# Layer B: emptying the key and query accumulators behind the next product's first two splits, and a second place for the LayerNorm rows

## The chip, the cores and the metric

The kernel runs on one core of one Trainium2 chip. A core has engines that work side by side, each through its own list of instructions in order: TensorE (PE, matrix products; PEld is its loading of weights), VectorE (DVE), ScalarE (ACT), GpSimd (POOL, all but unused here) and SyncE (SP, which issues the transfers from memory). They wait for one another through semaphores. The metric is the device time of one execution in microseconds (us), lower is better.

## The reference

A decoder trunk with two layers, 256 tokens and width 2048, all in 32-bit floats. Layer A is a state-space mixer. After it one set of keys and values is made from its output x; layer B is an attention with three head groups g, each with its own window and dilation, eight heads of 128 in each.

```python
k, v   = split(x @ kv_w)                  # 2048 -> 3072 keys, 3072 values
shift, scale, gate = split(silu(c) @ ada_w[1] + ada_b[1])   # 2048 -> 3 x 2048
h      = x * (1 + scale) + shift
q, z   = split(h @ b_in_w)                # 2048 -> 3072 queries, 1024 gate
o      = merge over g of softmax(q_g k_g' / sqrt(128) + alibi) v_g
out    = layer_norm(2**0.5 * x + (1 + gate) * ((o * silu(z)) @ b_out_w), ln_g, ln_b)
```

## The kernel before

**Products in split precision.** Every large product is computed as three: a weight piece `raw` (128 x 1024, 512 KB) is loaded, ACT copies it to a rounded high part `whi` (line 99), DVE subtracts to get the low part `wlo` (line 101), and PE multiplies high by high, high by low and low by high. There are six buffers for `raw`, four for `whi` and four for `wlo`.

**The stretch that the change touches** is the second half of the program.

- First come the values of the first half of the heads (`wv`, chunks of eight pieces by `tm_chunk`; evicted by `evict_v`, two ACT copies of 128 x 512, line 856).
- Then twelve key products (`wk`), each one call of `cm_wide`. It takes four pieces q = 0..3, called p0 to p3 below. A piece gives 16 matmuls: for each of four slices of the contraction two of 128 x 512 with the high part (line 173), then two of 128 x 256 with the low part (line 176). The results stand in a pair of PSUM accumulators `acc`; four accumulators exist, so one product fills a pair while the other pair is emptied. Emptying one takes an ACT copy (line 181) and a DVE addition (line 182), 128 x 256, and this twice per product.
- Then three more chunks of `wv`. Meanwhile the input of layer B, h, is made in place of x, tile by tile for 16 tiles (`htmp`: ACT line 923, DVE line 924; then the split into `actT`: ACT line 225, DVE line 226). A tile of x may only be overwritten when PE has read it for the last time, in the last `wv` chunk.
- Then six query products (`wbin`, `cm_wide` again), an attention over four heads, six more query products, the second attention, and the end.

**Background work.** `jobs` is a list from which `background` takes a job after a piece (`rate`). During keys and values every second piece takes one column of the adaLN matrix: a 1 MB load `araw` and a DVE dot product (line 279, two buffers). During the first queries each piece takes one step of `weigh` (line 943): the residual u is multiplied with the LayerNorm weight and then increased by the LayerNorm bias, for four column blocks n and two token blocks b. The rows of weight and bias for one n stand in one tile `pT` (128 x 1024), broadcast from memory by two transfers of 256 KB; the tile has one place, so the rows of n + 1 are loaded when n is done.

**What sets the order.** The functions write the instructions down; a scheduler then lays them out, engine by engine, by its own estimate of when each could start, so an instruction may come ahead of others that the code writes first. `tc.issue_after(x)` binds it: what is inside stands behind x. `upcoming`, `begin_next`, `first_or` and `behind_next` start the next product early: if `upcoming` holds its source, its p0 is loaded and split before the last piece of the running product, and the emptying stands behind that split. In layer A `upcoming` is filled; in layer B it is empty in this kernel, so `begin_next` does nothing there and `behind_next` binds nothing.

Of the kernel before, what the change touches and what calls it, by code (L numbers as in the profile page):

```python
# [9 lines left out]
F32 = mybir.dt.float32  # L10
F32R = mybir.dt.float32r
I32 = mybir.dt.int32
AF = mybir.ActivationFunctionType
# [5 lines left out]
P = 128  # L19
L = 256  # L20
D = 2048
# [6 lines left out]
NG = 3  # L28
# [21 lines left out]
def trunk(ctx, tc, xT, x, c, par, cst, bias, lnrow, ada, wdt, win, wxs, wout, wk, wv, wbin, wbout, out):  # L50
    nc = tc.nc
    V, S, T, PO = nc.vector, nc.scalar, nc.tensor, nc.gpsimd
# [9 lines left out]
    def bcast(dst, src, off=0):  # L62
        nc.sync.dma_start(dst, bass.AP(tensor=src.tensor, offset=src.offset + off,
                                       ap=[[0, P], [1, dst.shape[-1]]]))
# [37 lines left out]
        return hi.rearrange("p (k n) -> p k n", k=2), lo.rearrange("p (k n) -> p k n", k=2)  # L102

    jobs, latest, copied, pin = [], [], [], [None]
    upcoming, ready = [], []

    def first_or(src, q):

        return ready.pop() if ready else split(load_piece(src[q]))
# [7 lines left out]
    def behind_next():  # L117

        stack = ExitStack()
        if ready:  # L120
            stack.enter_context(tc.issue_after(copied[-1].ins))
            stack.enter_context(tc.issue_after(latest[-1].ins))
        return stack
# [34 lines left out]
            background(*rate)  # L158
        return ps

    def cm_wide(src, dst, rate=(0, 1), moving=None):

        both, high = moving or (lambda kt: xp[:, kt], lambda kt: xhi[:, kt, :])
        ps = acc_pair()
        for q in range(KT // 4):
            w = first_or(src, q)
            if q == KT // 4 - 1:
                begin_next()
            hi, lo = (t.rearrange("p k n -> p (k n)").rearrange("p (k n) -> p k n", k=4) for t in w)
            for k in range(4):  # L170
                kt = 4 * q + k
                for n in range(2):
                    T.matmul(ps[n], hi[:, k, n * P:n * P + P], both(kt), start=kt == 0, stop=False,  # L173
                             skip_group_check=True)
                for n in range(2):
                    T.matmul(ps[n][:, 0, :], lo[:, k, n * P:n * P + P], high(kt), start=False, stop=kt == KT - 1,  # L176
                             skip_group_check=True)
            background(*rate)
        with behind_next():
            for n in range(2):  # L180
                S.activation(dst[:, n, :], ps[n][:, 1, :], AF.Copy)
                V.tensor_tensor(dst[:, n, :], ps[n][:, 0, :], dst[:, n, :], op=ALU.add)

    def tiles(ps):
        return [ps[n // 2][:, n % 2, :] for n in range(4)]
# [20 lines left out]
    def tm_chunk(src, ahi, alo, nk=KT, rate=(0, 1), k0=0, pre=None, split_end=0):  # L206

        ps = tm_pair()
        n = nk // 2 - split_end
        for q in range(k0 // 2, n):  # L210
            if pre:
                pre(q)
            w = first_or(src, q)
            if q == nk // 2 - 1:
                begin_next()
            tm_piece(src, q, ps, ahi, alo, k0, nk, w=w)
            background(*rate)
        held = [(q, split(load_piece(src[q]))) for q in range(n, nk // 2)]
        for b in range(2):
            for q, w in held:  # L220
                tm_mults(q, w, ps, ahi, alo, k0, nk, (b,))
        return ps
# [63 lines left out]
    def gate_out(layer):  # L286

        ada_bias(layer, slice(0, KT), slice(2, 3))
        pt = aux.tile([P, 512], F32, name="aux")[:KT, :P]
        T.transpose(pt, mod[layer][:, :, 2], ident)  # L290
        row = sm.tile([KT, P], F32, name="row", bufs=1)
        V.tensor_copy(row, pt)
        nc.sync.dma_start(gated[layer].rearrange("(k p) -> k p", p=P), row)
# [24 lines left out]
    with ExitStack() as cA:  # L318
# [15 lines left out]
        with ExitStack() as cS:  # L334
# [78 lines left out]
            with ExitStack() as c0:  # L413
# [42 lines left out]
                for row in ("b4:0. b6:0. h z2:0. b2:0 x1:0 h", "b2:1. x1:1. z1:0 z1:1. z4:0 h h",  # L456
# [3 lines left out]
                    for w in row.split():  # L460
                        if w == two:
                            n = -2 if sum(o[0] == -2 for o in order) == sum(o[0] == -1 for o in order) else -1
# [99 lines left out]
            R = (1, 10)  # L562
# [284 lines left out]
    kv, vt = {}, {}  # L847
# [4 lines left out]

    def evict_v(hq, g, ps):
        vt[hq, g] = place(3 * hq + g if hq == 0 else 9 + g, [P, 2, 512])
        for b in range(2):
            S.activation(vt[hq, g][:, b, :], ps[b], AF.Copy)

    with ExitStack() as cL:
        pl = cL.enter_context(tc.tile_pool(name="pl", bufs=3))

        vps = [tm_pair(), tm_pair()]
        def high(i, b):
            for k in range(2):
                kt = 2 * (i // 2) + k
                for w in first_v[i]:
                    T.matmul(vps[i % 2][b], hx(kt)[:, b * P:b * P + P], w[:, k, :], start=kt == 0 and w is first_v[i][0],  # L866
                             stop=False)

        def low(i, b):
            for k in range(2):  # L870
                T.matmul(vps[i % 2][b], lx(2 * (i // 2) + k)[:, b * P:b * P + P], first_v[i][0][:, k, :], start=False,
                         stop=False)

        end, _ = x_quad(0)
        with tc.issue_after(end.ins):
            for n in range(1, 4):
                normalise(0, 512 * n, 512 * n + 512)
        for i in range(4):
            high(i, 0)
        for i in range(4):  # L880
            if i == 2:
                _, tile4 = x_quad(1)
                for n in range(1, 4):
                    normalise(1, 512 * n, 512 * n + 512)
            low(i, 0)
        for i in range(4):
            high(i, 1)
            if i == 2:
                x_tile(4)
                x_tile(5)  # L890
        for i in range(4):
            low(i, 1)
        for q in range(2, KT // 2):
            if q < KT // 2 - 1:
                x_tile(2 * q + 2)
                x_tile(2 * q + 3)
            for j in range(2):
                w = split(load_piece(wv[2 * j][q]), after=tile4.ins if q == 2 else None)
                tm_mults(q, w, vps[j], hx, lx, 0, KT, range(2))
        for g in range(2):  # L900
            evict_v(0, g, vps[g])

        R = (1, 2)
        pin[0] = latest[-1].ins
        with tc.issue_after(tile4.ins):
            state[0] = 0
            queue(pl, cols1[11:])
            jobs.append(lambda: gate_out(1))
            evict_v(0, 2, tm_chunk(wv[4], hx, lx, rate=R))
            for hq in range(2):  # L910
                for g in range(NG):
                    kv[hq, g] = place(3 + 3 * hq + g, [P, 4, L])
                    for w in range(2):
                        cm_wide(wk[2 * (2 * g + hq) + w], kv[hq, g][:, 2 * w:2 * w + 2, :], rate=R)
            for g in range(NG):
                evict_v(1, g, tm_chunk(wv[1 + 2 * g], hx, lx, rate=R))
            drain()
            late = latest[-1].ins

        ada_bias(1, slice(0, KT), slice(0, 2))  # L920
        for kt in range(KT):
            t = pl.tile([P, L], F32, name="htmp")
            S.activation(t, xhi[:, kt, :].bitcast(F32), AF.Identity, bias=shift(1, kt), scale=scale(1, kt))
            V.scalar_tensor_tensor(t, xlo[:, kt, :].bitcast(F32), scale(1, kt), t, op0=ALU.mult, op1=ALU.add)
            split_act(xhi[:, kt, :], xlo[:, kt, :], t)
    cQ = ctx.enter_context(ExitStack())
    pc2 = cQ.enter_context(tc.tile_pool(name="pc2", bufs=2))
# [4 lines left out]
    gmask = bs[:, CG:CG + 640]  # L932
    R = (0, 1)

    def weigh(n, b, i):
        if b == 0 and i == 0:
            t = pc2.tile([P, 1024], F32, name="pT", bufs=1)
            lnr[n] = [t[:, 512 * j:512 * j + 512] for j in range(2)]
            for j in range(2):
                bcast(lnr[n][j], lnrow, j * D + 512 * n)  # L940
        cs_ = slice(512 * n, 512 * n + 512)
        with tc.issue_after(late):
            V.tensor_tensor(u[b][:, cs_], u[b][:, cs_], lnr[n][i], op=(ALU.mult, ALU.add)[i])

    lnr = {}
    state[0] = 0
    jobs.extend(lambda n=n, b=b, i=i: weigh(n, b, i) for n in range(4) for i in range(2) for b in range(2))

    def queries(hq):
        qq = [pc2.tile([P, 4, L], F32, name=f"q{g}") for g in range(NG)]  # L950
        for g in range(NG):
            for w in range(2):
                cm_wide(wbin[2 * (2 * g + hq) + w], qq[g][:, 2 * w:2 * w + 2, :], rate=(1, 1))
        return qq

    def attend(hq, qq):
# [91 lines left out]
    for n in range(2):  # L1048
        ps = tm_chunk(wbout[n], *og, nk=H)
# [12 lines left out]
    ps = [tm_pair() for _ in range(2)]  # L1062
# [140 lines left out]
```

## Time and profile before

| | us |
|---|---|
| three runs, median (lowest to highest) | 1247.58 (1247.24 to 1248.12) |
| the profiled execution, its own time | 1247.47 |
| its span, first to last instruction | 1245.7 |
| PE busy | 1216.8 (98%) |
| PE weight loads busy | 1043.1 (84%) |
| DVE busy | 1029.4 (83%) |
| ACT busy | 702.5 (56%) |

The profiled execution is 0.11 us from the median, so numbers of its trace can be set against either. Times in the trace count from the start of the span. The stretch in question lies between 771 and 1041 us: keys to about 907, values to 974, first queries to 1041. A table by windows gives busy time of each engine in a stretch and the number of its instructions in brackets; an engine's timeline gives start, duration, line, operands and, in square brackets, the idle time just before and what ended it. In a timeline several equal instructions in a row are drawn together (x2), with one duration from the first start to the last end; consecutive matmuls overlap.

### The profile page before, as it was taken

Reading aid. Unit: us, or ns where it says so; the run is one execution under the profiler, and the core shown is the slowest. Engines: PE = TensorE matmul, PEld = TensorE weight load, DVE = VectorE, ACT = ScalarE, POOL = GpSimd, SP = SyncE. Lnnn points to the kernel's source line nnn. Section 1 sums busy time; section 2 is a strip of 40 time slices with the busy share of each in tenths; the row PEclk is TensorE's granted clock in tenths of the full one; section 3 lists DMA queues with packets and bytes.
Section 4 is the critical chain, followed back from the end, with each engine's and each line's share of the span. In section 5 each row is a group of like instructions: output and inputs, shape, how many; then the busy total and the mean of one; then the engine's idle time right before and its main releaser. Section 6 shows DMA issues by size and latency. Waiting matters only on the chain.

```text
span 1245.7 us, 18736 instructions
## 1 busy us (share of the span) xinstructions
PE 1216.8 (98%) x7086; PEld 1043.1 (84%) x7086; DVE 1029.4 (83%) x1454; ACT 702.5 (56%) x1045; POOL 0.2 (0%) x4
## 2 busy tenths in 40 slices
PE   4999999999999999999999999999999999999997
PEld 4989998898888888888888788888888888888886
DVE  6999986999987989899768678879888867658777
ACT  3645477868597789654335554443445644445631
POOL 0000000000000000000000000000000000000000
PEclk9999999999999999999999999999999999999999
DMA  9999977687556456699998569988998774463751
GB/s 381 422 421 422 421 266 252 223 287 263 211 186 220 155 183 194 227 334 351 337 333 288 187 213 375 363 329 344 354 382 314 238 242 135 136 204 117 232 175 67
DMA packets 80586, 335.88 MB, mean 270 GB/s; under 512 B 9104, under 2 KB 9328, under 8 KB 67696
## 3 DMA queue, kind: packets, MB, share of 16 engines
q1 hardware_dynamic: 80496, 334.69, 74.6%
q8 instruction: 55, 0.90, 0.3%
q14 instruction: 35, 0.29, 0.1%
HBM read 332.47 MB, written 2.18 MB: 269 GB/s over the span
## 4 chain that ended last, share of the span: by engine, by line
PE 86%; DVE 6%; DMA 4%; ACT 2%; issue 2%; SPq 0%; DVEq 0%; ACTq 0%
PE acc L173 21%; PE acc L199 12%; PE acc L200 12%; PE acc L198 12%; PE acc L176 11%; PE acc L144 3%; PE acc L146 3%; PE acc L145 3%; DMA araw<-in_ada 2%; DVE araw L279 2%; DVE wlo L101 2%; PE py L657 1%; ACT whi L99 1%; PE acc L866 1%; PE aux L969 1%
## 5 line engine op out<-in xcount | busy, mean ns | idle before, releaser
L99 ACT ACTIVATE whi<-raw 128x1024 fp32r<-128x1024 f32 x392 | 411.2, 1058 | 369.9 <-PE acc L200 135.9
L101 DVE TENSOR_TENSOR wlo<-raw,whi 128x1024 fp32r<-128x1024 f32 x392 | 472.7, 1220 | 135.9 <-ACT whi L99 128.5
L173 PE MATMUL acc<-actT,whi 128*128 128x512 f32 x1280 | 405.3, 397 | 0.0
L176 PEld LDWEIGHTS acc<-actT,wlo 128*128 128x128 f32 x1280 | 239.1, 188 | 59.1 <-DVE wlo L101 4.3
L199 PE MATMUL acc<-wlo,actT 128*128 128x512 f32 x656 | 257.5, 393 | 0.6 <-DVE wlo L101 0.5
L176 PE MATMUL acc<-actT,wlo 128*128 128x256 f32 x1280 | 253.4, 279 | 1.7 <-DVE wlo L101 1.2
L198 PE MATMUL acc<-whi,actT 128*128 128x512 f32 x656 | 253.1, 394 | 0.0
L279 DVE SCALAR_TENSOR_TENSOR araw<-araw,cb__72 128x2048 f32<-128x2048 f32 x96 | 219.3, 2285 | 12.1 <-DMA araw<-in_ada 11.8
L173 PEld LDWEIGHTS acc<-actT,whi 128*128 128x128 f32 x1280 | 195.9, 189 | 0.4
L200 PE MATMUL acc<-whi,actT 128*128 128x512 f32 x432 | 168.9, 391 | 0.0
L199 PEld LDWEIGHTS acc<-wlo,actT 128*128 128x128 f32 x656 | 123.2, 188 | 28.0 <-DVE wlo L101 3.1
L198 PEld LDWEIGHTS acc<-whi,actT 128*128 128x128 f32 x656 | 122.5, 188 | 24.2
L144 PE MATMUL acc<-actT,whi 128*128 128x256 f32 x384 | 109.1, 288 | 17.6 <-ACT actT L446 17.4
L145 PE MATMUL acc<-actT,whi 128*128 128x256 f32 x384 | 109.4, 287 | 0.0
L146 PE MATMUL acc<-actT,wlo 128*128 128x256 f32 x384 | 107.5, 287 | 0.9 <-DVE wlo L101 0.9
L200 PEld LDWEIGHTS acc<-whi,actT 128*128 128x128 f32 x432 | 81.1, 188 | 16.6
L144 PEld LDWEIGHTS acc<-actT,whi 128*128 128x128 f32 x384 | 74.5, 195 | 18.6 <-ACT actT L446 17.6
L200 PE MATMUL acc<-whi,ylo 128*128 128x512 f32 x224 | 87.6, 391 | 0.0
L145 PEld LDWEIGHTS acc<-actT,whi 128*128 128x128 f32 x384 | 75.1, 196 | 0.3
L146 PEld LDWEIGHTS acc<-actT,wlo 128*128 128x128 f32 x384 | 73.9, 196 | 1.3 <-DVE wlo L101 1.3
L200 PEld LDWEIGHTS acc<-whi,ylo 128*128 128x128 f32 x224 | 42.1, 188 | 8.5
L615 ACT ACTIVATE seg<-cbc,cumT 128x128 f32<-128x128 f32 x128 | 41.0, 389 | 4.9 <-DVE wlo L101 2.3
(273 smaller groups left out, 1108.8 us busy)
## 6 DMA issues: line engine op xcount, KB each, us to landing
araw<-in_ada SPq DMA_DIRECT2D x96, 1024.0 KB, 7.5
raw<-in_win SPq DMA_DIRECT2D x112, 512.0 KB, 6.8
raw<-in_wout SPq DMA_DIRECT2D x64, 512.0 KB, 5.8
raw<-in_wbin SPq DMA_DIRECT2D x64, 512.0 KB, 3.7
raw<-in_wxs SPq DMA_DIRECT2D x48, 512.0 KB, 4.6
raw<-in_wv SPq DMA_DIRECT2D x48, 512.0 KB, 6.7
raw<-in_wk SPq DMA_DIRECT2D x48, 512.0 KB, 7.1
cbc<-cumd SPq DMA_DIRECT2D x16, 512.0 KB, 4.7
```

The lines of the kernel that those rows point to most:

```text
L99: copied.append(S.activation(hi, raw, AF.Copy))
L101: latest.append(V.tensor_tensor(lo, raw, hi.bitcast(F32), op=ALU.subtract))
L144: T.matmul(o, hi[:, k, c_], ahi[:, kt, :], start=first, stop=False, skip_group_check=True)
L145: T.matmul(o, hi[:, k, c_], alo[:, kt, :], start=False, stop=False, skip_group_check=True)
L146: T.matmul(o, lo[:, k, c_], ahi[:, kt, :], start=False, stop=kt == k1 - 1, skip_group_check=True)
L173: T.matmul(ps[n], hi[:, k, n * P:n * P + P], both(kt), start=kt == 0, stop=False, skip_group_check=True)
L176: T.matmul(ps[n][:, 0, :], lo[:, k, n * P:n * P + P], high(kt), start=False, stop=kt == KT - 1, skip_group_check=True)
L198: T.matmul(o, h_, hi[:, k, :], start=kt == k0, stop=False, skip_group_check=part)
L199: T.matmul(o, h_, lo[:, k, :], start=False, stop=False, skip_group_check=part)
L200: end = T.matmul(o, l_, hi[:, k, :], start=False, stop=kt == k1 - 1, skip_group_check=part)
L279: V.scalar_tensor_tensor(raw, raw, 1.0, cb_, op0=ALU.mult, op1=ALU.mult, accum_out=mod[layer][:, ct, j:j + 1])
L615: S.activation(seg[:, hh, b, :], cbc[:, hh, b, :], AF.Relu, bias=cumT[:, b, h0 + hh:h0 + hh + 1], scale=-1.0)
```

## The change

**Emptying.** `cm_wide` gets `later`. With it, the emptying of the accumulators is not written at the end of the product but put in a list `owed`; `settle` writes it in the next product, after the split of its second piece (p1), bound behind the last ACT copy and the last DVE subtraction written so far. The twelve key products and all queries but the last of each half are `later`. `upcoming` is filled for keys, values and queries, so the next product's p0 is split before the last piece of the running one. `evict_v` is bound behind the split that was begun ahead.

**LayerNorm rows.** `fetch` loads the rows of block n: even n into `pT`, odd n into the score tiles `sc0` and `sc1` of the attention that follows (128 x 512 each). The rows of n + 1 are asked for in the second step of block n, so two blocks' rows can stand side by side. One job (`fetch(0)`) is added ahead.

```diff
@@ settle, new
+    upcoming, ready, owed = [], [], []
+
+    def settle():
+
+        while owed:
+            with tc.issue_after(copied[-1].ins), tc.issue_after(latest[-1].ins):
+                owed.pop(0)()
@@ cm_wide
             w = first_or(src, q)
+            if q == 1:
+                settle()
             if q == KT // 4 - 1:
                 begin_next()
...
-        with behind_next():
+        def put():
             for n in range(2):
                 S.activation(dst[:, n, :], ps[n][:, 1, :], AF.Copy)
                 V.tensor_tensor(dst[:, n, :], ps[n][:, 0, :], dst[:, n, :], op=ALU.add)
+
+        if later:
+            owed.append(put)
+        else:
+            with behind_next():
+                put()
@@ tm_chunk
             w = first_or(src, q)
+            if q == 1:
+                settle()
@@ evict_v
-        for b in range(2):
-            S.activation(vt[hq, g][:, b, :], ps[b], AF.Copy)
+        with behind_next():
+            for b in range(2):
+                S.activation(vt[hq, g][:, b, :], ps[b], AF.Copy)
@@ keys and values
+            upcoming.extend((wk[2 * (2 * g + hq) + w], 0) for hq in range(2) for g in range(NG) for w in range(2))
+            upcoming.extend((wv[1 + 2 * g], 0) for g in range(NG))
...
-                        cm_wide(wk[2 * (2 * g + hq) + w], kv[hq, g][:, 2 * w:2 * w + 2, :], rate=R)
+                        cm_wide(wk[2 * (2 * g + hq) + w], kv[hq, g][:, 2 * w:2 * w + 2, :], rate=R, later=True)
@@ LayerNorm rows
-    def weigh(n, b, i):
-        if b == 0 and i == 0:
+    def fetch(n):
+        if n % 2 == 0:
             t = pc2.tile([P, 1024], F32, name="pT", bufs=1)
             lnr[n] = [t[:, 512 * j:512 * j + 512] for j in range(2)]
-            for j in range(2):
-                bcast(lnr[n][j], lnrow, j * D + 512 * n)
+        else:
+            lnr[n] = [pc2.tile([P, 512], F32, name=f"sc{j}", bufs=1) for j in range(2)]
+        for j in range(2):
+            bcast(lnr[n][j], lnrow, j * D + 512 * n)
+
+    def weigh(n, b, i):
+        if b == 1 and i == 0 and n < 3:
+            fetch(n + 1)
...
+    jobs.append(lambda: fetch(0))
@@ queries
+        upcoming.extend([(wbin[2 * (2 * g + hq) + w], 0) for g in range(NG) for w in range(2)][1:])
...
-                cm_wide(wbin[2 * (2 * g + hq) + w], qq[g][:, 2 * w:2 * w + 2, :], rate=(1, 1))
+                cm_wide(wbin[2 * (2 * g + hq) + w], qq[g][:, 2 * w:2 * w + 2, :], rate=(1, 1),
+                        later=(g, w) != (NG - 1, 1))
```

The order of instructions moves at three places on which the prediction rests. In the rows, numbers are buffer numbers; line numbers behind the edit are higher by 8 to 28 in the changed kernel (line 182 is 190, 279 is 295, 99 and 101 stay).

*First place: a key product, DVE.* Here one key product has just been finished (its accumulators `acc_8155` and `acc_8156`, in the changed kernel 8157 and 8158, are to be emptied into `s6`) and the next one starts. Before, DVE's rows are: subtraction for p0 of the next product, emptying, p1, a column of adaLN (`araw`), p2, p3, a column:

```order
L101 TENSOR_TENSOR wlo_8260<-raw_8257,whi_8259 128x1024
L182 TENSOR_TENSOR s6_8154<-acc_8155,s6_8154 128x256
L182 TENSOR_TENSOR s6_8154<-acc_8156,s6_8154 128x256
L101 TENSOR_TENSOR wlo_8282<-raw_8279,whi_8281 128x1024
L279 SCALAR_TENSOR_TENSOR araw_8301,mod1_85<-araw_8301,cb__72 128x2048
L101 TENSOR_TENSOR wlo_8307<-raw_8304,whi_8306 128x1024
L101 TENSOR_TENSOR wlo_8329<-raw_8326,whi_8328 128x1024
L279 SCALAR_TENSOR_TENSOR araw_8348,mod1_85<-araw_8348,cb__72 128x2048
```

Now they are: p0 of the next product (`wlo_8235`), a column, p1 (`wlo_8278`), emptying, a column, p2, p3, and already p0 of the product after that (`wlo_8335`):

```order
L101 TENSOR_TENSOR wlo_8235<-raw_8232,whi_8234 128x1024
L295 SCALAR_TENSOR_TENSOR araw_8254,mod1_85<-araw_8254,cb__72 128x2048
L101 TENSOR_TENSOR wlo_8278<-raw_8275,whi_8277 128x1024
L190 TENSOR_TENSOR s6_8156<-acc_8157,s6_8156 128x256
L190 TENSOR_TENSOR s6_8156<-acc_8158,s6_8156 128x256
L295 SCALAR_TENSOR_TENSOR araw_8301,mod1_85<-araw_8301,cb__72 128x2048
L101 TENSOR_TENSOR wlo_8307<-raw_8304,whi_8306 128x1024
L101 TENSOR_TENSOR wlo_8329<-raw_8326,whi_8328 128x1024
L101 TENSOR_TENSOR wlo_8335<-raw_8332,whi_8334 128x1024
```

The subtraction of p1 has moved ahead of the emptying, on ACT its copy likewise. In the kernel before, the emptyings of the first to fifth key product already stand behind the splits of p0 and p1 of the next (the first even behind p3), and those of the sixth to twelfth behind p0 alone, as above; now all twelve stand behind p1 or later.

*Second place: from the values to the queries, ACT.* `whi_9336` is the high part of p0 of the first query product; it stood just ahead of the split of tile 8 of h (tiles count from 0 to 15, `htmp_9276` is tile 8; rows of ACT before):

```order
L99 ACTIVATE whi_9336<-raw_9334 128x1024
L225 ACTIVATE actT_6987<-htmp_9276 128x256
L225 ACTIVATE actT_6987<-htmp_9281 128x256
L923 ACTIVATE htmp_9286<-actT_6987,mod1_85 128x256
L923 ACTIVATE htmp_9291<-actT_6987,mod1_85 128x256
L923 ACTIVATE htmp_9296<-actT_6987,mod1_85 128x256
L225 ACTIVATE actT_6987<-htmp_9286 128x256
L225 ACTIVATE actT_6987<-htmp_9291 128x256
L225 ACTIVATE actT_6987<-htmp_9296 128x256
L923 ACTIVATE htmp_9301<-actT_6987,mod1_85 128x256
L923 ACTIVATE htmp_9306<-actT_6987,mod1_85 128x256
L923 ACTIVATE htmp_9311<-actT_6987,mod1_85 128x256
```

and now stands behind tile 13 (`htmp_9301`), the place that p1 had; `b11` is the emptying of the last value chunk:

```order
L942 ACTIVATE htmp_9301<-actT_6987,mod1_85 128x256
L942 ACTIVATE htmp_9306<-actT_6987,mod1_85 128x256
L942 ACTIVATE htmp_9311<-actT_6987,mod1_85 128x256
L241 ACTIVATE actT_6987<-htmp_9301 128x256
L99 ACTIVATE whi_9336<-raw_9334 128x1024
L241 ACTIVATE actT_6987<-htmp_9306 128x256
L99 ACTIVATE whi_9361<-raw_9359 128x1024
L873 ACTIVATE b11_9232<-acc_9085 128x512
L873 ACTIVATE b11_9232<-acc_9086 128x512
L241 ACTIVATE actT_6987<-htmp_9311 128x256
```

The split of p0 has moved behind five more tiles, and p1 behind one more. PE's rows put the first query matmul right behind the last one of the value chunk, before and now.

*Third place: the LayerNorm rows on SP's queue,* at the start of the queries, before:

```order
L930 DMA bs_9323<-in_bias 128x1024
L63 DMA pT_9356<-in_lnrow 128x512 x2
L93 DMA raw_9536<-in_wbin 128x1024
L93 DMA raw_9562<-in_wbin 128x1024
L93 DMA raw_9585<-in_wbin 128x1024
L63 DMA pT_9457<-in_lnrow 128x512 x2
L93 DMA raw_9608<-in_wbin 128x1024
```

and now:

```order
L949 DMA bs_9323<-in_bias 128x1024
L63 DMA pT_9356<-in_lnrow 128x512 x2
L63 DMA sc0_9404<-in_lnrow 128x512
L63 DMA sc1_9405<-in_lnrow 128x512
L93 DMA raw_9516<-in_wbin 128x1024
L93 DMA raw_9558<-in_wbin 128x1024
L63 DMA pT_9506<-in_lnrow 128x512 x2
L93 DMA raw_9585<-in_wbin 128x1024
L63 DMA sc0_9607<-in_lnrow 128x512
L93 DMA raw_9612<-in_wbin 128x1024
L63 DMA sc1_9608<-in_lnrow 128x512
L93 DMA raw_9618<-in_wbin 128x1024
```

Two blocks' rows are asked for at once; of the later rows each pair or single row has fewer weight pieces between it and the next. From the second half of the queries on, the rows of all engines stand as before.

More of the change, by code (lines that the diff above doesn't have):

```diff
@@ L104, in trunk @@
     jobs, latest, copied, pin = [], [], [], [None]
-    upcoming, ready = [], []
+    upcoming, ready, owed = [], [], []
[3 more added lines that the diff above has]
+                owed.pop(0)()
     def first_or(src, q):
@@ L159, in cm_quad, with cm_wide @@
         return ps
-    def cm_wide(src, dst, rate=(0, 1), moving=None):
+    def cm_wide(src, dst, rate=(0, 1), moving=None, later=False):
         both, high = moving or (lambda kt: xp[:, kt], lambda kt: xhi[:, kt, :])
```

## The prediction

> **What bounds the kernel now.** I read the page first, then the waits of the second half, then busy time by windows, then the engines' timelines at one key product. The page says that PE is the bound nearly everywhere:
>
> ```profile
> PE 1216.8 (98%) x7086; PEld 1043.1 (84%) x7086; DVE 1029.4 (83%) x1454; ACT 702.5 (56%) x1045; POOL 0.2 (0%) x4
> ```
>
> So an edit that leaves PE its instructions can only win time in which PE waits or runs slower than it could. I cut the edited part into equal pieces of work: six key products, the other six, the three value chunks, six query products. The columns are the window, its length, busy time and count of PE, PEld, DVE, ACT and POOL, granted clock, transfer share, GB/s.
>
> ```profile
> 771.20:837.50 66.30, 66.30 (x383) 57.82 (x382) 52.75 (x54) 25.78 (x33) 0.00 (x0) 1.00 0.92 352
> 837.50:907.50 70.00, 68.32 (x385) 57.75 (x384) 60.26 (x64) 28.78 (x39) 0.00 (x0) 1.00 0.91 354
> 974.20:1041.00 66.80, 66.80 (x385) 58.26 (x384) 45.52 (x57) 30.16 (x38) 0.00 (x0) 1.00 0.75 236
> ```
>
> The same 385 matmuls of the same forms take 66.80 us in the queries and 70.00 in the second six key products: 3.20 us are lost there at an unchanged clock. The first six keys and the queries lose nothing. A free product takes 66.80/6 = 11.13 us. The waits between 837 and 938 us (who waited for what; total, times, longest) name the cause:
>
> ```profile
> ACT s L181 <- PE acc L176: 23.3, 5, 5.8
> DVE s L182 <- ACT s L181: 7.5, 5, 2.6
> PEld acc L176 <- DVE wlo L101: 4.3, 6, 1.4
> ```
>
> PE's weight load waits six times for a low part, and the engines that make the parts spend their time waiting at the emptying. The timelines of DVE, ACT and PE at one seam show how:
>
> ```profile
> 846.81 1.22 DVE L101 TENSOR_TENSOR wlo<-raw,whi 128x1024 fp32r<-128x1024 f32 x1
> 849.31 0.76 DVE L182 TENSOR_TENSOR s<-acc,s 128x256 f32<-128x256 f32 x2 [1.28 <-ACT s L181]
> 850.53 1.23 DVE L101 TENSOR_TENSOR wlo<-raw,whi 128x1024 fp32r<-128x1024 f32 x1 [0.47 <-ACT whi L99]
> 851.67 2.29 DVE L279 SCALAR_TENSOR_TENSOR araw<-araw,cb__72 128x2048 f32<-128x2048 f32 x1
> 853.88 2.36 DVE L101 TENSOR_TENSOR wlo<-raw,whi 128x1024 fp32r<-128x1024 f32 x2
> ...
> 848.89 0.66 ACT L181 ACTIVATE s<-acc 128x256 f32<-128x256 f32 x2 [5.27 <-PE acc L176]
> 849.44 2.96 ACT L99 ACTIVATE whi<-raw 128x1024 fp32r<-128x1024 f32 x3
> ...
> 848.81 0.63 PE L173 MATMUL acc<-actT,whi 128*128 128x512 f32 x2
> 854.15 0.40 PE L176 MATMUL acc<-actT,wlo 128*128 128x256 f32 x2
> 854.39 0.63 PE L173 MATMUL acc<-actT,whi 128*128 128x512 f32 x2
> 855.16 0.51 PE L176 MATMUL acc<-actT,wlo 128*128 128x256 f32 x2
> 855.50 0.63 PE L173 MATMUL acc<-actT,whi 128*128 128x512 f32 x2
> ```
>
> The new product starts at 848.81. ACT has stood 5.27 us at the emptying, and p1's copy is behind it; so DVE idles 1.28 us, empties, idles 0.47, subtracts p1, does a column, and only then p2. PE reaches p2 at 854.39; elsewhere the low part's matmul follows after 0.47 us, so at 854.86. It comes at 855.16: 0.30 late, and the next pair follows after 0.34 instead of 0.23, 0.11 more. That is 0.41 per product, and this seam has nothing unusual.
>
> **The change part by part.**
>
> *Emptying behind p1 (keys).* Instructions are the same, only their places differ. In the new order p1's split is done while the old product still runs, so from the seam on DVE has: emptying, column, p2. With the durations above: the emptying starts at 849.31 as before (PE's end sets it) and ends 850.07; the column, 2.21 from its start to the next start, ends 852.28; p2, 1.15 of the pair, ends 853.43. It is due at 854.86: 1.4 us of room instead of a wait. ACT has copied p2 by 849.55 + 1.0, before DVE asks. The kernel shows this very order once, where its scheduler already had p1 ahead of the fifth emptying:
>
> ```profile
> 826.60 0.76 DVE L182 TENSOR_TENSOR s<-acc,s 128x256 f32<-128x256 f32 x2 [1.43 <-ACT s L181]
> 827.27 2.28 DVE L279 SCALAR_TENSOR_TENSOR araw<-araw,cb__72 128x2048 f32<-128x2048 f32 x1
> 829.48 2.35 DVE L101 TENSOR_TENSOR wlo<-raw,whi 128x1024 fp32r<-128x1024 f32 x2
> ```
>
> and that stands in the window that loses nothing. One product of the second six also carries three steps of h on DVE, and PE stood longest there (1.4 in the waits). In the new order two of them stand ahead of p2; at 0.48 us each,
>
> ```profile
> 861.56 0.48 DVE L924 SCALAR_TENSOR_TENSOR htmp<-actT,mod,htmp 128x256 f32<-128x256 f32 x1
> ```
>
> 1.4 - 2 x 0.48 leaves 0.4 us of room. DVE's load per product is 4 x 1.15 + 2 x 2.21 + 0.76 = 9.8 us of 11.13, so it keeps up. Gain: all of the 3.20 us. The later emptying costs nothing: the pair is needed only when the product after the running one starts, a whole 11 us on. Bounds: 0 if something else is late next (the first rival), 3.2.
>
> *The last key product into the first value chunk.* The seam is the same; PE's rows there are
>
> ```profile
> 912.86 0.39 PE L200 MATMUL acc<-whi,actT 128*128 128x512 f32 x1
> 913.08 0.61 PE L198 MATMUL acc<-whi,actT 128*128 128x512 f32 x2
> 913.80 0.50 PE L199 MATMUL acc<-wlo,actT 128*128 128x512 f32 x1
> 914.14 0.39 PE L200 MATMUL acc<-whi,actT 128*128 128x512 f32 x1
> ```
>
> At 0.23 per matmul two take 0.46; the row comes after 0.72, and the next after 0.34: 0.26 + 0.11 = 0.37. I take 0.4 as gained.
>
> *Emptying of the value chunks (`evict_v` bound).* It stood behind the next p0 already and still does, with p1 behind it; nothing gained at the second chunk, nothing lost. Bounds: 0 to the 0.4 of one such seam.
>
> *p0 of the first query product moves down on ACT and DVE.* The rows of before at that place:
>
> ```profile
> 971.04 1.57 ACT L923 ACTIVATE htmp<-actT,mod 128x256 f32<-128x256 f32 x3
> 972.52 0.40 ACT L225 ACTIVATE actT<-htmp 128x256 fp32r<-128x256 f32 x1
> 972.82 1.05 ACT L99 ACTIVATE whi<-raw 128x1024 fp32r<-128x1024 f32 x1
> ...
> 973.90 1.23 DVE L101 TENSOR_TENSOR wlo<-raw,whi 128x1024 fp32r<-128x1024 f32 x1 [0.44 <-ACT whi L99]
> ...
> 974.23 0.61 PE L173 MATMUL acc<-actT,whi 128*128 128x512 f32 x2
> 974.68 0.40 PE L176 MATMUL acc<-actT,wlo 128*128 128x256 f32 x2
> ```
>
> The split in these rows is p1's, early by more than 2 us. In the new order p0's stands in its place; if it runs at the same distance from PE, its low part ends at 973.90 + 1.15 = 975.05, due at 974.68: 0.37 late. A split fewer among the tiles ahead (1.05 on ACT) could make it earlier, but these tiles wait for PE's last reading of x, which moves with PE. Bounds 0 and 0.8 (with the slow second pair, and one more ACT step ahead); I take 0.3, near the row.
>
> *LayerNorm rows.* DVE waited 7.6 us for them, but ACT's splits waited for PE to free a buffer, not for data, and PE lost nothing in the window above: the time won here is worth 0. (Waits between 940 and 1050; then the query loads, issue to landing, 955 to 1000.)
>
> ```profile
> DVE u L943 <- DMA pT<-in_lnrow: 7.6, 8, 2.0
> ACT whi L99 <- PE acc L173: 35.0, 22, 1.7
> ...
> raw<-in_wbin SPq DMA_DIRECT2D x16, 512.0 KB, 6.1
> ```
>
> *Queries' emptying.* It moves behind p1 as well; where nothing is lost nothing is won: 0.
>
> Sum: -3.2 - 0.4 + 0.3 = -3.3 us. The profiled execution took 1247.47, so 1244.2; the median is 0.11 higher, which I leave out.
>
> **The rivals.** A measurement here tells about 0.2% (2.5 us) from no change, so faster means under 1245.1 and slower over 1250.1.
>
> *Transfers take the place of the wait.* A key product loads four pieces of 512 KB and two columns of 1 MB, 4.19 MB; in 11.13 us that is 377 GB/s, and now p1's data must be there before the emptying may run. Best rate over a stretch of this length here, at a transfer share of 0.96:
>
> ```profile
> 907.45:929.74 22.29, 22.18 (x98) 17.83 (x97) 19.03 (x18) 9.23 (x11) 0.00 (x0) 1.00 0.96 370
> ```
>
> At 370 a product takes 11.33 us, twelve 136.0 against the 136.3 of the two windows: keys gain 0.3 instead of 3.2, and the time is 1247.1. Against it: the page shows slices far above 377 where nothing holds the queue back,
>
> ```profile
> GB/s 381 422 421 422 421 266 252 223 287 263 211 186 220 155 183 194 227 334 351 337 333 288 187 213 375 363 329 344 354 382 314 238 242 135 136 204 117 232 175 67
> ```
>
> and the loads wait for buffers, which the new order frees earlier. For it: both key windows moved only 352 and 354, the first by living on what was loaded ahead. Were 354 a ceiling and not what was asked for, a product would take 11.84 us, twelve 142.0, 5.7 more than now, and the time would be 1253.1; the same slices of 421 and 422 leave that 0.02.
>
> The Trainium skill (DMA: Bandwidth & Descriptors, Where 436 GB/s comes from) holds such a ceiling: loads from memory are bound at about 358 GB/s per core, by which the twelve products would need 140.5 us and the kernel about 1251, an estimate from that page. The 422 in the slices of this profile does not agree with it.
>
> *A query piece behind a LayerNorm row.* SP takes its queue in order, and a row's load waits for `weigh` to free its tile; a piece behind it starts late. Now four rows stand ahead of the third product's p0, and single rows between single pieces. If one piece is asked for so late that PE waits through its whole landing, 6.1 us, the time is 1244.2 + 6.1 = 1250.3, slower. It decides once a piece lands later than PE frees its buffer; the 22 waits for PE above say that there was room at each piece.
>
> *More than reckoned.* If h's tiles also run ahead and the second value chunk's seam closes, 0.3 + 0.4 more: 1243.5; with the slow pairs at all three chunks 1243.0.
>
> **How the numbers follow.** My forecast has 0.60, more than reckoned 0.10, transfers at 370 GB/s 0.20, a ceiling at 354 0.02, the query piece 0.08. Faster is the first two, 0.70; same 0.20; slower 0.10. Time 1244.2. The range runs from 1242.8, under the best case, to 1247.1, the transfer rival; the two slow cases stay outside.
>
> **What would show it.** Right: 385 matmuls of the second six keys in about 66.8 us, no weight load of line 184 waiting for `wlo`, emptying on DVE directly followed by a column, a short wait at the first query's low part. Wrong: ACT copies of p1 waiting for `raw<-in_wk` ahead of an emptying, with PE waiting at p2 as before; or ACT's query copies waiting for `raw<-in_wbin`.

## The result, and the profile after

| | before | after |
| --- | --- | --- |
| time, median of 7 runs each (us) | 1247.58 (1246.67 to 1249.06) | 1243.95 (1243.14 to 1244.69) |
| profiled execution: time, span (us) | 1247.47, 1245.7 | 1243.86, 1242.1 |

The ratio after to before is 0.9967, with a 95% interval of 0.9958 to 0.9977: faster by a third of a per cent, which is more than a measurement here can miss. The forecast was 1244.2.

The engines' totals and the rates of transfer in the 40 slices of the page after:

```profile
PE 1214.3 (98%) x7086; PEld 1043.6 (84%) x7086; DVE 1029.0 (83%) x1454; ACT 703.7 (57%) x1045; POOL 0.2 (0%) x4
GB/s 383 422 421 422 421 268 242 222 302 252 210 200 205 169 167 206 208 337 355 353 322 291 190 201 382 347 341 362 384 381 297 230 256 133 137 205 117 234 173 68
```

The counts of instructions are those of before. DVE and ACT are as busy as they were; PE's busy time is shorter by 2.5 us, since the records count part of a wait for a low part as busy (68.32 in the window of the second six keys before, for work that takes 66.80).

The windows of after, for six key products, the other six, and six query products (window, length, busy time and count of PE, PEld, DVE, ACT, POOL, granted clock, transfer share, GB/s):

```profile
771.10:837.40 66.30, 66.30 (x383) 57.86 (x382) 54.77 (x55) 26.95 (x34) 0.00 (x0) 1.00 0.91 345
837.40:904.20 66.80, 66.80 (x386) 58.28 (x385) 59.88 (x64) 29.90 (x39) 0.00 (x0) 1.00 0.98 373
970.36:1037.20 66.84, 66.84 (x383) 58.05 (x383) 46.09 (x58) 30.74 (x39) 0.00 (x0) 1.00 0.76 243
```

The second row is the one that counts. It was 70.00 us for 385 matmuls, and is 66.80 for 386, as much as six query products took before, which lost nothing. One seam between two key products, in the timelines of DVE, ACT and PE after (lines 181, 184, 189, 190 and 295 here are 173, 176, 181, 182 and 279 of before):

```profile
849.07 0.76 DVE L190 TENSOR_TENSOR s<-acc,s 128x256 f32<-128x256 f32 x2 [1.43 <-ACT s L189]
849.74 2.28 DVE L295 SCALAR_TENSOR_TENSOR araw<-araw,cb__72 128x2048 f32<-128x2048 f32 x1
851.95 3.49 DVE L101 TENSOR_TENSOR wlo<-raw,whi 128x1024 fp32r<-128x1024 f32 x3
...
848.65 0.66 ACT L189 ACTIVATE s<-acc 128x256 f32<-128x256 f32 x2 [3.98 <-PE acc L184]
...
848.57 0.63 PE L181 MATMUL acc<-actT,whi 128*128 128x512 f32 x2
854.14 0.63 PE L181 MATMUL acc<-actT,whi 128*128 128x512 f32 x2
854.61 0.40 PE L184 MATMUL acc<-actT,wlo 128*128 128x256 f32 x2
```

The new product starts at 848.57. The emptying on DVE is followed by the column without a gap, then by p2. P2's low part takes 1.15 of the three in its row and is done at 853.10; PE uses it at 854.61, 0.47 after the high part, without waiting. There are 1.5 us of room where before there were 0.30 too few.

The waits of after between 728 and 1050 us that concern weights and LayerNorm rows (who waited for what; total, times, longest):

```profile
ACT whi L99 <- DMA raw<-in_wk: 16.6, 10, 3.9
...
DVE u L968 <- DMA pT<-in_lnrow: 1.6, 2, 1.3
...
DVE u L968 <- DMA sc<-in_lnrow: 1.3, 1, 1.3
...
PEld acc L213 <- DVE wlo L101: 0.7, 1, 0.7
...
PEld acc L184 <- DVE wlo L101: 0.4, 1, 0.4
```

Of the six waits for a low part in the keys none is left. The two that remain lie at the second value chunk and at the first query. ACT waits for key weights in transfer ten times, 16.6 us in all, where before it did so four times, 7.7 us; these waits end early enough that PE does not see them. DVE's waits for LayerNorm rows are down from 7.6 us to 2.9. The first query's place, in the timelines of ACT, DVE and PE:

```profile
968.60 1.05 ACT L99 ACTIVATE whi<-raw 128x1024 fp32r<-128x1024 f32 x1
...
969.67 1.23 DVE L101 TENSOR_TENSOR wlo<-raw,whi 128x1024 fp32r<-128x1024 f32 x1 [0.44 <-ACT whi L99]
...
970.40 0.61 PE L181 MATMUL acc<-actT,whi 128*128 128x512 f32 x2
...
970.96 0.50 PE L184 MATMUL acc<-actT,wlo 128*128 128x256 f32 x2
971.30 0.62 PE L181 MATMUL acc<-actT,whi 128*128 128x512 f32 x2
```

The low part comes 0.56 after the high part in place of 0.47, and the next pair after 0.34 in place of 0.23: 0.20 us lost. The queries begin at 970.40 in place of 974.23, 3.83 earlier; less these 0.20 that is the 3.6 by which the span is shorter.

### The profile page after: what moved, and what is told of

It reads as the page before. It is cut to its first block, busy times and chain, and to the rows that moved or that the text cites. A ratio compares the mean times of both kernels' runs of the same rounds, so it can differ in the third digit from the quotient of the medians.

```text
span 1242.1 us, 18728 instructions
## 1 busy us (share of the span) xinstructions
PE 1214.3 (98%) x7086; PEld 1043.6 (84%) x7086; DVE 1029.0 (83%) x1454; ACT 703.7 (57%) x1045; POOL 0.2 (0%) x4
## 4 chain that ended last, share of the span: by engine, by line
PE 89%; DVE 4%; DMA 3%; ACT 2%; issue 1%; SPq 0%; DVEq 0%; ACTq 0%
PE acc L181 24%; PE acc L213 12%; PE acc L214 12%; PE acc L212 12%; PE acc L184 12%; PE acc L150 3%; PE acc L152 3%; PE acc L151 3%; DMA araw<-in_ada 2%; PE py L673 1%; DVE wlo L101 1%; DMA raw<-in_wv 1%; ACT whi L99 1%; PE acc L883 1%; PE aux L726 1%
```

## The experiments

Ratios are to runs of the kernel before on the same chip. "Stall" is what PE's start times show beyond the regular spacing, with the slower pair behind it.

**The parts of the change, each alone.** First the keys' part, with the rows and queries of before; then the rest, with the keys of before.

```
 keys alone:   cm_wide(wk[...], ..., rate=R, later=True)   and the list for wk, wv, the bound in evict_v
 rest alone:   fetch(n), two places for the rows; queries' list and later=...
```

> The keys' part of the change alone: the later emptying of the key products, the list of the pieces to begin early for keys and values, and the bound on the value chunks' emptying. LayerNorm rows and queries stand as before the change. Theory (the low part of each key product's third piece came 0.41 us too late because emptying and column stood ahead of it on VectorE): all of the gain is here, 1243.9 to 1244.2 us, ratio 0.997 to before. Rival (the second place for the LayerNorm rows, or the queries' emptying, gave the gain): 1247.3 to 1247.6, ratio 1.000.

> The rest of the change alone: second place for the LayerNorm rows, the queries' list and later emptying; key products and value chunks as before the change. Theory: nothing, 1247.3 to 1247.8 us, ratio 1.000, the 70.00 us stretch of the second six key products stays. Rival (rows or queries gave the gain): 1243.9 to 1244.5.

Measured: the keys' part 1245.80 us (1243.63 to 1248.23, 11 runs), ratio 0.9984 (0.9975 to 0.9992); the rest 1247.56, ratio 0.9997 (0.9988 to 1.0006). In the profile of the rest the second six keys still take 70.00 us:

```profile
837.60:907.60 70.00, 68.31 (x385) 57.70 (x384) 60.25 (x64) 29.29 (x39) 0.00 (x0) 1.00 0.96 356
```

So rows and queries alone give nothing, as expected. But neither expectation fits the keys' part: it keeps only half of the gain, and its runs spread over 4.6 us. Its key stalls are gone, all six; in the queries there is a new one, 2.23 us. DVE, PE and SP's queue there:

```profile
1007.58 0.69 DVE L962 TENSOR_TENSOR u<-u,pT 128x512 f32<-128x512 f32 x1 [4.68 <-DMA pT<-in_lnrow]
1008.19 1.22 DVE L101 TENSOR_TENSOR wlo<-raw,whi 128x1024 fp32r<-128x1024 f32 x1
...
1009.46 0.50 PE L184 MATMUL acc<-actT,wlo 128*128 128x256 f32 x2 [1.97 <-DVE wlo L101]
...
1001.79 0.80 SPq L63 DMA_DIRECT2D pT<-in_lnrow  x2
```

DVE stands 4.68 us at a LayerNorm row in transfer, and the low part that PE needs is behind it. With one place the fourth row's load can be issued only when the third row is used up, at 1001.79, so it lands 5.8 us later. Two runs ask which part of the change keeps this away: one puts the rows' part back, the other the queries'.

```
 keys and rows:      upcoming.extend([(wbin...)...]) and later=... taken out of queries()
 keys and queries:   fetch(n) taken out, rows fetched at weigh(n, 0, 0) into pT alone
```

> The change without its queries' part (no list of query pieces to begin early, each query product emptied at its end as before): the keys' part and the second place for the LayerNorm rows stay. The run of the keys' part alone gave 1245.80 us in place of 1243.95, with one stall of 2.23 us at a query piece whose low part stood on VectorE behind a LayerNorm row that was still in transfer (4.68 us of waiting). Theory A (the second place for the rows is what keeps that stall away once the queries begin 3.8 us earlier): no such stall, 1243.7 to 1244.3. Theory B (the queries' list and later emptying keep it away): the stall is there, 1245.2 to 1246.4.

> The change without its LayerNorm part (one place for the rows, each fetched when the one before is used up): the keys' and the queries' parts stay. Theory A (the second place keeps the stall away): a query piece waits behind a row in some of the runs, 1245.2 to 1246.4 us with a wide spread, as in the keys' part alone. Theory B (the queries' part keeps it away): 1243.7 to 1244.3.

Measured: keys and rows 1243.94 us (1243.38 to 1245.44), ratio 0.9963 (0.9949 to 0.9977); keys and queries 1246.73 (1244.93 to 1247.56), ratio 0.9987 (0.9978 to 0.9996). Theory A holds, though the second time lies a little above its range: the second place for the rows is needed, the queries' part does nothing that can be measured. In the trace of keys and queries DVE waits for rows and PE for low parts:

```profile
DVE u L962 <- DMA pT<-in_lnrow: 11.3, 6, 3.7
PEld acc L184 <- DVE wlo L101: 3.1, 3, 1.5
```

The same kernel as the keys' part alone, but with three of the four row loads left out (all sixteen row operations use the first pair), takes the suspected wait away directly:

```diff
     def weigh(n, b, i):
-        if b == 0 and i == 0:
+        if n:
+            lnr[n] = lnr[0]
+        elif b == 0 and i == 0:
```

> The keys' part alone (LayerNorm rows with one place, queries as before the change), but only the first of the four pairs of rows is loaded and all sixteen row operations use it: three row loads of 512 KB are left out, and with them the waits of rows two to four. The keys' part alone gave 1245.80 us and, with the first query piece begun early, 1247.97. Theory (a row that is still in transfer stands on VectorE ahead of a query piece's low part, and that is all that the keys' part alone loses): 1243.6 to 1244.3. Rival (the row waits only show it; the queries lose because they begin 3.8 us earlier against the rest of their own loads): 1245 to 1247.5.

Measured: 1243.54 us (1243.23 to 1245.55), ratio 0.9963 (0.9950 to 0.9977). Its waits between 970 and 1045:

```profile
DVE u L964 <- DMA pT<-in_lnrow: 2.5, 2, 2.0
PEld acc L184 <- DVE wlo L101: 0.4, 1, 0.4
```

This run leaves out the loads as well as the waits for them; keys and rows, which keeps all four loads and loses nothing either, shows that the loads by themselves cost nothing that can be measured. So the row waits were all that the keys' part alone lost.

That raises a question which I could not settle: the kernel before has one place as well and loses nothing there. What differs is when the fourth row's load is issued, counted from the first query matmul: 27.7 us in before (1001.97 less 974.23), 31.4 in the keys' part alone (1001.79 less 970.43), 32.5 in keys and queries, and 20.1 for the last one in the change. The lag of the keys' part alone behind before is there from the first row: counted from the first query matmul, its four rows are issued 0.9, 2.2, 2.1 and 3.6 us later (973.28, 983.11, 991.16 and 1001.79 against 976.21, 984.73, 992.81 and 1001.97). I took the order of loads on SP's queue for the reason and brought it near that of before:

```diff
             upcoming.extend((wv[1 + 2 * g], 0) for g in range(NG))
+            upcoming.append((wbin[0], 0))
```

> The keys' part alone (rows with one place, queries as before the change), and the first query piece is begun early, which puts two more query pieces ahead of the first row's load on the load queue, as in the kernel before, and leaves two or three pieces between the later rows' loads (three and four in the keys' part alone). The keys' part alone gave 1245.80 us, the keys' and queries' parts 1246.73. Theory C (what costs is where rows and pieces stand to each other on the load queue and on VectorE, not the earlier start): 1243.3 to 1244.5. Theory D (with one place the rows come too late as soon as the queries begin 3.8 us earlier, in whatever order): 1245 to 1247.

Measured: 1247.97 us (1245.41 to 1250.11, 11 runs), ratio 0.9993 (0.9984 to 1.0002). The time lies outside the range of theory C, but this run is no clean test of it, because the edit moved the rows on DVE too: the fourth row stands ahead of the low part of the 13th query piece here, and ahead of that of the 14th in before and in the keys' part alone. It is issued 30.1 after the first matmul (1001.53 less 971.48). PE stalls 2.43 us at that piece, and for 3.41 us right behind the stall its granted clock is 0.50, so that the matmuls there take twice their time, about 1.7 us more:

```profile
1008.47 0.80 PE L184 MATMUL acc<-actT,wlo 128*128 128x256 f32 x2 [2.26 <-DVE wlo L101]
```

```profile
1008.37:1011.78 3.41, 3.31 (x11) 2.92 (x12) 3.41 (x6) 0.00 (x0) 0.00 (x0) 0.50 0.54 154
```

The stall of 2.23 us in the keys' part alone has no such stretch in its trace; why the clock fell in the one and not in the other is not shown. Theory D is not safe either: the kernel with short columns below also has one place and starts its queries at 970.13, with the order of before; its fourth row goes out after 28.3 us, and it loses only 0.52 at a query. Late rows cost; how much of their lateness comes from the earlier start, and how much from the order on the queue and on DVE, stays open.

**The place of the emptying.** The whole change, but key products are emptied behind the next product's first piece:

```diff
-   cm_wide(wk[...], kv[hq, g][...], rate=R, later=True)
+   cm_wide(wk[...], kv[hq, g][...], rate=R)
```

> The whole change, except that a key product is emptied behind the split of the next product's first piece alone; pieces are begun early as in the change. On VectorE some seven of the twelve products then have the order emptying, second piece, column, third piece again. Theory (the place of the emptying decides): the stalls at the third piece are back in about seven products, 7 x 0.41 = 2.9 us, so 1246.5 to 1247.2 us; more if a column in front of the emptying holds it up too. Rival (what gained was that first pieces are loaded and split early, not where the emptying stands): 1243.9 to 1244.3.

Measured: 1248.09 us (1246.99 to 1249.29, 11 runs), ratio 1.0001 (0.9992 to 1.0010): all of the gain is lost (1246.5 to 1247.2 was expected), and the list of pieces begun early is worth nothing without the later emptying. A seam of this kernel, DVE and then PE:

```profile
850.73 0.76 DVE L190 TENSOR_TENSOR s<-acc,s 128x256 f32<-128x256 f32 x2 [1.30 <-ACT s L189]
851.95 1.23 DVE L101 TENSOR_TENSOR wlo<-raw,whi 128x1024 fp32r<-128x1024 f32 x1 [0.47 <-ACT whi L99]
853.09 2.29 DVE L295 SCALAR_TENSOR_TENSOR araw<-araw,cb__72 128x2048 f32<-128x2048 f32 x1
855.30 3.49 DVE L101 TENSOR_TENSOR wlo<-raw,whi 128x1024 fp32r<-128x1024 f32 x3
...
856.58 0.50 PE L184 MATMUL acc<-actT,wlo 128*128 128x256 f32 x2 [0.15 <-DVE wlo L101]
```

Emptying, p1, column, p2, and the stall of 0.42 is back, at the same six seams as in before and in nearly the same sizes (five times 0.41 to 0.43, and 1.31, in before 1.22, where steps of h stand on DVE too), 3.4 us; a seventh of 0.53 at the first value chunk makes 3.9. I had expected 2.9, with seven equal stalls.

**The column ahead of p2.** The kernel before, with shorter columns:

```diff
-   V.scalar_tensor_tensor(raw, raw, 1.0, cb_, ...)
+   n = 256 if layer and kv else D
+   V.scalar_tensor_tensor(raw[:, :n], raw[:, :n], 1.0, cb_[:, :n], ...)
```

> The kernel before, with each modulation column that is computed during the value chunks and key products of layer B taken over the first 256 of its 2048 elements (seven eighths of these dot products are left out; all loads stay, and so does the order around the emptyings). Theory (VectorE's queue ahead of the third piece's low part is too long by 0.30 us, and the column of about 2.2 us is the longest thing in it): a column of some 0.3 us takes the stalls away though the emptying stays where it was, 66.8 us for the second six key products, 1243.4 to 1244.4 us, ratio 0.997. Rival (the key products wait for their transfers at about 370 GB/s, and the order on VectorE only shows it): nothing, 1247.3 to 1247.6, since the loads are the same.

Measured: 1243.64 us (1243.03 to 1244.26), ratio 0.9967 (0.9954 to 0.9979). Its second six key products, and a seam on DVE:

```profile
837.40:904.20 66.80, 66.80 (x386) 58.28 (x385) 38.10 (x64) 28.55 (x39) 0.00 (x0) 1.00 0.94 367
```

```profile
848.90 0.75 DVE L183 TENSOR_TENSOR s<-acc,s 128x256 f32<-128x256 f32 x2 [4.60 <-ACT s L182]
850.12 1.23 DVE L101 TENSOR_TENSOR wlo<-raw,whi 128x1024 fp32r<-128x1024 f32 x1 [0.47 <-ACT whi L99]
851.27 0.42 DVE L281 SCALAR_TENSOR_TENSOR araw<-araw,cb__72 128x256 f32<-128x256 f32 x1
851.61 0.09 DVE L281 DVE_READ_ACCUMULATOR araw<-araw,cb__72 128x1 f32 x1
851.61 2.36 DVE L101 TENSOR_TENSOR wlo<-raw,whi 128x1024 fp32r<-128x1024 f32 x2
```

The emptying stands where it stood in before, the loads are the same, the column takes 0.42 in place of 2.29, and every key stall is gone. It is the length of DVE's queue ahead of p2, not the transfers, that held PE.

**How much room the transfers have.** The change, with a spare load of 256 or 512 KB beside each key product, which nothing reads; the load is issued right behind the product's next piece (for 512 KB, 1024 in place of 512):

```diff
+   extra.append(lambda s=wout[hq][2 * g + w][:, :512]: nc.sync.dma_start(
+       pl.tile([P, 512], F32, name="aside", bufs=2), s))
    cm_wide(wk[2 * (2 * g + hq) + w], kv[hq, g][...], rate=R, later=True)
```

> The change, and each of the twelve key products loads 256 KB of another weight beside its own (4 pieces of 512 KB and about two columns of 1 MB, 4.19 MB), which nothing reads. In 11.07 us a product asks for 402 GB/s in place of 379. Theory (the key products have room in their transfers; the order on VectorE was what cost): 1243.8 to 1244.4 us. Rival (transfers hold at about 380 GB/s in this stage, so that the change has just reached the next bound): 4.46 MB at 380 GB/s are 11.73 us, 12 x 0.66 = 7.9 us more, about 1252.

> The same with 512 KB beside each key product: 4.72 MB, 426 GB/s, which is above the fullest slice of the page (422). Theory: here the transfers become the bound by little: 4.72 MB at 422 GB/s are 11.18 us, 12 x 0.11 = 1.3 us more, 1244.5 to 1247. Rival (about 380 GB/s): 12.4 us a product, 16 us more, about 1260.

Measured: 1243.49 us (1243.17 to 1244.27), ratio 0.9964 (0.9951 to 0.9978), and 1244.39 (1243.90 to 1245.06), ratio 0.9971 (0.9959 to 0.9983). The two windows of six key products with 512 KB beside each:

```profile
771.20:837.40 66.20, 66.20 (x382) 57.77 (x381) 54.49 (x55) 27.00 (x34) 0.00 (x0) 1.00 0.98 394
837.40:904.00 66.60, 66.60 (x382) 57.70 (x381) 59.21 (x62) 29.50 (x39) 0.00 (x0) 1.00 1.01 409
```

409 GB/s for 66.6 us, and no more than three spacings of 0.1 us too long to be seen on PE in these windows. So the rival at 380 GB/s is out, and both times lie a little under their expected ranges. The windows of the second run moved 394 and 409 GB/s and not 426, since a product of the change moves about 4.0 MB (345 and 373 GB/s in its two windows) where 4.19 were reckoned. But the second window's transfer share is 1.01, and the highest rate over a longer stretch that a trace here shows is not far above it; in before, at a share of 1.02:

```profile
31.14:155.71 124.57, 123.86 (x831) 114.74 (x830) 116.71 (x125) 68.37 (x90) 0.00 (x0) 1.00 1.02 421
```

The 373 of the change lie 48 under these 421, the 409 only 12. No run here asks for more than that.

**The seams that are left.** The change, with the three value chunks emptied behind p1 of the next product; then that, and the first query piece begun early.

```diff
-        with behind_next():
+        def put():
             for b in range(2):
                 S.activation(vt[hq, g][:, b, :], ps[b], AF.Copy)
+        if hq:
+            owed.append(put)
+        else:
+            with behind_next():
+                put()
```

and in the second of the two also

```diff
             upcoming.extend((wv[1 + 2 * g], 0) for g in range(NG))
+            upcoming.append((wbin[0], 0))
```

> The change, and the three value chunks behind the key products are emptied behind the next product's second piece too, as the key products are. In the trace of the change one seam is left among these chunks: 0.49 + 0.11 = 0.60 us at the second piece of the second chunk, and 0.08 at the third. Theory (place of the emptying decides here too, on ScalarE, where two copies stand between the high parts of the first and the second piece): 0.6 us less, 1243.2 to 1243.5. Rival (the second piece's low part is held by something else, its load or the column): nothing, 1243.8 to 1244.2.

> The run before this one, and the first query piece is loaded and split early, in front of the last tiles of the second modulation. Theory: the 0.20 us that the change's trace shows at the first query's low part goes as well, 1243.0 to 1243.3. Rival (the piece in front of the last tiles makes those tiles late, by up to its own 1.05 us on ScalarE and 1.23 us on VectorE): 1243.5 to 1244.5.

Measured: 1243.56 us (1243.17 to 1244.88), ratio 0.9964 (0.9951 to 0.9976), and 1243.14 (1242.72 to 1243.62), ratio 0.9959 (0.9946 to 0.9971). In the first the stall of the second chunk is gone, but the first query, which starts earlier, loses 0.52 in place of 0.20 (its low part was late on DVE: 970.13 below, 0.88 after the high part):

```profile
969.25 0.61 PE L181 MATMUL acc<-actT,whi 128*128 128x512 f32 x2
970.13 0.50 PE L184 MATMUL acc<-actT,wlo 128*128 128x256 f32 x2 [0.27 <-DVE wlo L101]
```

In the second both are gone: from the keys to the end of the queries' products PE shows no spacing over 0.1 us too long.

```profile
970.19 0.62 PE L181 MATMUL acc<-actT,whi 128*128 128x512 f32 x2
970.64 0.40 PE L184 MATMUL acc<-actT,wlo 128*128 128x256 f32 x2
```

Its median is 0.8 us under that of the change, which is what the two stalls were worth; the intervals of the two ratios overlap, so the trace carries this more than the times do.

## Why the prediction was right, and where it was not

- **Emptying behind p1, -3.2.** Right in place, mechanism and size: the window went from 70.00 to 66.80 us, all six stalls went, with 1.5 us of room where 1.4 was worked out. Moving only the emptying back brought the stalls back; shortening only the column took them away from before.
- **Last key product into the first value chunk, -0.4.** Right: 913.80 had 0.37 in before, and after shows nothing there.
- **Emptying of the value chunks, 0.** Right: the stall of the second chunk was 0.57 in two pieces and is 0.60 in one, its low part behind a column on DVE.
- **First query piece behind tile 13, +0.3.** 0.20, by the row's working: 0.09 late and 0.11 for the slow pair.
- **LayerNorm rows, 0 ("the time won here is worth 0").** This step failed, though the sum did not show it. I took the term from before's window, where PE lost nothing, and that holds for the rows alone (1247.56). But the other terms move the queries 3.8 us earlier and shift the loads on SP's queue; without the second place a row is then late enough to hold a query piece's low part, and 1.9 to 2.8 us of the 3.6 are lost (1245.80 and 1246.73 against 1243.95; 2.1 and 2.5 by the ratios). The rows' part is the cover under which the keys' gain is kept. What I left out was the other side of the question: what rows that are not moved would cost against queries that are. That the sum came out even so is luck in this term, since the change holds the part that the argument took to be worth nothing.
- **Queries' emptying, 0.** Right: 1243.94 without it.
- **Transfers at 370 GB/s (1247.1) and at 354 (1253.1).** Both wrong. 370 was what the stage asked for, not what it could have; 394 and 409 ran at no loss that can be measured. The amount, 4.19 MB a product, was too high as well: about 4.0 in the trace of the change. (The estimate of about 1251 for a ceiling at 358 comes to 1251.6 when it is added up like the 1253.1.) The Trainium skill (DMA: Bandwidth & Descriptors, Where 436 GB/s comes from) gives about 358 GB/s as the bound of loads from memory; these windows disagree. Another page of the Trainium skill (Perfetto Trace Analysis, Roofline) calls that figure the share when both cores of a pair load, and takes about 120% of it as the practical ceiling of a single one, an estimate of 430 from that page; 409 and the slices of 422 agree with it.
- **A query piece behind a LayerNorm row (1250.3).** It did not come in the change: its rows are all on their way 20.1 us after the first query matmul. But it is the very wait that the keys' part alone shows, at 2.23 us in place of 6.1, because the row there is late by part of its landing only. The rival named the mechanism and put it on the wrong kernel.

## What to carry to other kernels

At a seam between two accumulations, list what each in-order engine has between the end of the old product and the first operand of the new one that is not ready, and compare its sum with the time at which PE reaches that operand; here 0.30 us too much cost PE 0.41 us at each such seam, behind an engine that was busy 83% of the span. A part of a change that is worth nothing against the kernel before can still be what keeps the other part's gain, so cost each part also as the one that is missing.

## What the runs showed that I had not expected

- One core loaded 409 GB/s over 66.6 us beside a PE that was busy throughout, and 55 GB/s more than this stage had moved before (354) cost nothing measurable. The trace of before could have told that much: it moves 421 GB/s over 124.57 us in which PE is busy for 123.86.
- The keys' part alone spread over 4.6 us (11 runs) and, with the first query piece begun early, over 4.7 us, where the kernel before spread over 2.7 to 3.1 on the four chips of these experiments. That the landing of the late row differs from run to run may be the reason, but each kernel has one trace, and keys and queries, where PE waits for rows too, spread over 2.6 only. The clock may have a part in it: the half-clock stretch above cost its execution about 1.7 us, and of the 11 runs of that kernel the four under 1246 us had a mean granted clock of 0.998 or 0.999, while six of the seven above 1247 had 0.996 or 0.997.
